# Softmax reciprocals taken before they are spread, and every low part subtracted on VectorE

## The chip, the cores and the metric

The kernel runs on one core of one Trainium2 chip. The metric is the device time of the program in microseconds; a profiled execution has besides its time a span, from the first to the last instruction of its trace. TensorE multiplies matrices, VectorE, ScalarE and GpSimd work on tiles in SBUF, and SyncE issues the loads.

## The reference

Two blocks follow each other on 256 tokens of width 1024, all in float32. The first has two layers over 256 latent and 256 context tokens. Each normalises, projects with `w_in`, runs three branches side by side (a gated MLP over chunks, an attention with 8 query and 2 key heads, and a two-way mLSTM scan), and projects with `w_out`. The second block has two layers too: an attention of 16 heads (`moba`) or a low-rank attention of 16 heads (`mla`), each followed by a feed-forward part with a short convolution.

```python
def _attend(q, k, v):
    s = jnp.einsum('bqkgd,bskd->bkgqs', q, k).astype(jnp.float32) * ATTN_SCALE
    p = jax.nn.softmax(s, axis=-1).astype(v.dtype)
    return jnp.einsum('bkgqs,bskd->bqkgd', p, v)
...
def conv_ffn(xn, w_gate, conv_w, conv_b, w_up, w_down):
    S = xn.shape[1]
    g = xn @ w_gate
    gp = jnp.pad(g, ((0, 0), (CONV_WIDTH - 1, 0), (0, 0)))
    gc = conv_b + sum(conv_w[j] * gp[:, j:j + S] for j in range(CONV_WIDTH))
    h = jax.nn.gelu(gc, approximate=False) * (xn @ w_up)
    return h @ w_down
```

## The kernel before

Activations lie transposed: features on the 128 partitions, tokens along the free axis, as eight tiles (`KT`) of 128 features. Each product of float32 matrices is made of three matmuls in a shorter format. `split` (L130) makes the high part of a tile by a cast on ScalarE and the low part by subtracting that cast from the tile, and `mm3` (L105) or `stream_on` (L120) adds high by high, low by high and high by low in one accumulator.

Weights come in pieces of up to 128x1024 by `fetch` (L145): `w_load` loads a piece into `st` (four buffers), and `w_split` makes `wh` on ScalarE and `wl`, the low part (five buffers each). `fetch` takes a key and looks it up in the table `POOL_LO` (L58). The table's digits say which pieces of that fetch have their low part subtracted on GpSimd; all others, and every fetch without a key, have it on VectorE. The feed-forward stages (`ffn`, L1320) fetch without a key.

In attention a softmax weight is left undivided. `attend` (L782) in the first block and `weights_of` (L1032) in the second take the exponentials and, with the same ScalarE instruction, their sums, one column per head, into `dn`. The division comes after the product with the values: `inv_rows` (L293) makes the reciprocals, repeated 64 times along the free axis, so that transposes on TensorE turn them into rows that lie like the heads' outputs. It is called 12 times in the first block with four heads (128x256), and eight times by `out_heads` (L1064) with eight columns (128x512). `out_heads` then copies the rows from PSUM, multiplies, and splits the heads' output; that split's low part is on GpSimd.

The order of the work in a stage is written out by hand in the strings of `PLAN` (L46), one letter and number for a step. On top of it the framework schedules the recorded instructions anew when the program is built, by a model of the engines' times, and each engine then runs its own list strictly in order. So a change of one instruction's engine shifts rows on all engines. The residual additions are L915 and L1083, the square sums L274, the output products' next splits L921 and L1006; the scan of the gate statistics is L610 and L613, the rope products L492 and L497.

Of the kernel before, what the change touches and what calls it, by code (L numbers as in the profile page):

```python
# [28 lines left out]
def _cols(*spans):  # L29
# [26 lines left out]
}  # L56

POOL_LO = {"g00": "1", "g03": "1", "g04": "01", "g05": "0", "g10": "1", "g11": "1", "g12": "1", "g13": "01",  # L58
# [4 lines left out]

FWD = [2, 3, 0, 1]
BWD = [3, 2, 1, 0]
# [3 lines left out]
def tile_two_blocks(ctx: ExitStack, tc: tile.TileContext, A, out, dbg=None):  # L69
    nc = tc.nc  # L70
    V, S, G, PE = nc.vector, nc.scalar, nc.gpsimd, nc.tensor
# [9 lines left out]
    def bank(tag):  # L81
        return psum.tile([128, 512], F32, name=tag)
# [47 lines left out]
    def split(hi, lo, src, lo_eng=None):  # L130
        S.copy(hi, src)  # L131
        (lo_eng or V).tensor_tensor(lo, src, hi.bitcast(F32), op=OP.subtract)  # L132

    def w_load(src):
        st = wpool.tile([128, src.shape[-1]], F32, name="st", bufs=4)
        load(st, src)
        return st

    def w_split(st, on_pool):
        hi = wpool.tile(list(st.shape), F32R, name="wh", bufs=5)  # L140
        lo = wpool.tile(list(st.shape), F32R, name="wl", bufs=5)
        split(hi, lo, st, G if on_pool else V)
        return hi, lo

    def fetch(src, pieces, key=None):  # L145
        r, a = [], 0
        for i, p in enumerate(pieces):
            r.append(w_split(w_load(src[:, a:a + p]), str(i) in POOL_LO.get(key, "")))
            a += p
# [5 lines left out]
    def transpose(o, i):  # L155
        last_tr[0] = PE.transpose(o, i, ident[:i.shape[0], :i.shape[0]]).ins  # L156
# [136 lines left out]
    def inv_rows(rr, cols):  # L293

        n = cols.shape[-1]
        rr = rr[:, :n * 64].rearrange("p (a b) -> p a b", b=64)
        V.reciprocal(rr, cols.unsqueeze(2).to_broadcast([128, n, 64]))  # L297
        pt = bank("tr")
        for p in range(n // 2):
            transpose(pt[:, p * 128:(p + 1) * 128], rr[:, 2 * p:2 * p + 2, :].rearrange("p a b -> p (a b)"))  # L300
        return pt[:, :n * 64]
# [9 lines left out]
    def first_layer(l, ncx, x, rc):  # L311
# [470 lines left out]
        def attend(t, i):  # L782
# [38 lines left out]
            if p:  # L821
                oj = obs[t][:, j * 256:(j + 1) * 256]
                S.copy(oj, inv_rows(T2(), dn[:, j * 4:j * 4 + 4]))
                V.tensor_tensor(oj, po[j][:, :256], oj, op=OP.mult)
# [144 lines left out]
    x, rc = first_layer(0, True, x0, None)  # L969
# [94 lines left out]
    def out_heads(sb, po, dn, oh, ol, g):  # L1064

        pt = inv_rows(sb.tile([128, 512], F32, name="rr2", bufs=1), dn[:, 8 * g:8 * g + 8])
        o = sb.tile([128, 2, 256], F32, name="ov", bufs=2)
        of = o.rearrange("p a b -> p (a b)")
        S.copy(of, pt)
        V.tensor_tensor(of, po, of, op=OP.mult)  # L1070
        split(oh[:, 2 * g:2 * g + 2, :], ol[:, 2 * g:2 * g + 2, :], o, G)

    def w_o_proj(name, src, oh, ol, first, nrm):
        w = first
# [12 lines left out]
    def moba(hh, hl, rc):  # L1087
# [68 lines left out]
        oh = sb2.tile([128, 8, 256], F32R, name="moh")  # L1156
        ol = sb2.tile([128, 8, 256], F32R, name="mol")
        steps["o"] = lambda g: out_heads(sb, ov[g], dn, oh, ol, g)
        for f_ in late_.split():
            steps[f_[0]](int(f_[1:]))  # L1160
# [6 lines left out]
    def mla(nrm):  # L1167
# [139 lines left out]
        def value_heads(g):  # L1307
            ov[g] = values_of(PTs, va, 4 * g)

        steps = {"k": keys_of, "q": queries_w, "h": weights, "u": lambda i: values(i, wv[i]), "v": value_heads,  # L1310
                 "o": lambda g: out_heads(sb, ov[g], dn, oh, ol, g)}
        for f_ in PLAN["mla"].split():
            steps[f_[0]](int(f_[1:]))
# [191 lines left out]
```

## Time and profile before

| | |
|---|---|
| median of 3 runs | 1150.46 us (1150.42 to 1152.39) |
| profiled execution | 1150.56 us, span 1148.8 us |
| TensorE busy | 1096.8 us, 95% of the span |
| VectorE busy | 772.9 us, 67% |
| ScalarE busy | 596.6 us, 52% |
| GpSimd busy | 295.6 us, 26% |
| weight low parts on VectorE | 211 instructions, 250.0 us |
| weight low parts on GpSimd | 61 instructions, 140.7 us |

TensorE is busy in nearly all of the span, so the table says little about where time can be won or lost; that is read from single waits. Busy times are of one execution. A busy TensorE is not always TensorE at its full clock.

### The profile page before, as it was taken

To read this page: it belongs to the slowest core of one execution; us is meant where nothing else is said; L and a number is where in the kernel's file an instruction comes from. 1 tells how busy PE (TensorE), PEld (TensorE's weight loads), DVE (VectorE), ACT (ScalarE), POOL (GpSimd) and SP (SyncE) were. 2 spreads that over 40 slices of the span, in tenths; PEclk is the share of its full clock that TensorE was granted. 3 is DMA by queue.
4 is the path that set the end of the run, shared out by engine and by line. 5 is a ranking of instruction groups with operands and counts; after the bars stand their busy time and mean duration, and the time that the engine had idled before them with its cause. 6 is when DMAs were issued, how large, how long until landed. Compare 5 with 4: busy or idle time off the path is not lost. (4 is left out here: it accounts for less than half of the span.)

```text
span 1148.8 us, 20497 instructions
## 1 busy us (share of the span) xinstructions
PE 1096.8 (95%) x7826; PEld 960.6 (84%) x7826; DVE 772.9 (67%) x1525; ACT 596.6 (52%) x1158; POOL 295.6 (26%) x283
## 2 busy tenths in 40 slices
PE   5999989999899899988999999999999989999997
PEld 3686777687677799887876899999998889999996
DVE  4774574666646766877576777776556877777653
ACT  4446543443435475554456565555447856555541
POOL 1350321321212725334222312221032331222100
PEclk9999999999899999999999999999999999999998
DMA  9624310534742243124442355556545325555561
GB/s 337 242 83 148 129 55 1 184 128 167 229 141 88 73 132 121 65 98 152 165 140 81 122 173 188 187 181 182 175 143 171 112 91 175 194 185 184 178 183 45
DMA packets 52610, 167.32 MB, mean 146 GB/s; under 512 B 6816, under 2 KB 10400, under 8 KB 52512
## 3 DMA queue, kind: packets, MB, share of 16 engines
q1 hardware_dynamic: 52512, 166.01, 43.4%
q8 instruction: 62, 1.02, 0.3%
q14 instruction: 36, 0.29, 0.1%
HBM read 164.41 MB, written 1.05 MB: 144 GB/s over the span
## 5 line engine op out<-in xcount | busy, mean ns | idle before, releaser
L131 ACT CAST wh<-st 128x1024 fp32r<-128x1024 f32 (+4 forms) x272 | 268.7, 992 | 202.4 <-PE acc L100 112.6
L132 DVE TENSOR_TENSOR wl<-st,wh 128x1024 fp32r<-128x1024 f32 (+4 forms) x211 | 250.0, 1187 | 110.6 <-ACT wh L131 106.2
L132 POOL TENSOR_TENSOR wl<-st,wh 128x1024 fp32r<-128x1024 f32 (+4 forms) x61 | 140.7, 2317 | 272.3 <-ACT wh L131 246.3
L100 PE MATMUL acc<-xyh,wh 128*128 128x512 f32 (+1 forms) x320 | 112.1, 351 | 6.3 <-DVE xres L915 4.4
L100 PE MATMUL acc<-xyl,wh 128*128 128x512 f32 (+1 forms) x320 | 111.3, 350 | 2.6 <-DVE xyl L132 2.6
L100 PE MATMUL acc<-xyh,wl 128*128 128x512 f32 (+1 forms) x320 | 111.1, 348 | 0.0
L100 PE MATMUL acc<-wh,xyh 128*128 128x512 f32 (+1 forms) x256 | 96.6, 377 | 4.9 <-DVE t L497 3.5
L100 PE MATMUL sc<-hl,wh 128*128 128x256 f32 x352 | 99.0, 281 | 0.0
L100 PE MATMUL sc<-hh,wl 128*128 128x256 f32 x352 | 99.0, 281 | 0.0
L100 PE MATMUL acc<-hl,wh 128*128 128x256 f32 x352 | 99.0, 281 | 0.0
L100 PE MATMUL acc<-ah,wh 128*128 128x256 f32 x352 | 99.0, 281 | 0.0
L100 PE MATMUL acc<-al,wh 128*128 128x256 f32 x352 | 99.0, 281 | 0.0
L100 PE MATMUL acc<-ah,wl 128*128 128x256 f32 x352 | 98.9, 281 | 0.0
L100 PE MATMUL sc<-hh,wh 128*128 128x256 f32 x352 | 98.9, 281 | 0.0
L100 PE MATMUL acc<-hh,wh 128*128 128x256 f32 x352 | 98.8, 281 | 0.0
L100 PE MATMUL acc<-hh,wl 128*128 128x256 f32 x352 | 98.8, 281 | 0.0
L100 PE MATMUL acc<-wh,xyl 128*128 128x512 f32 (+1 forms) x256 | 94.8, 370 | 0.0
L100 PE MATMUL acc<-wl,xyh 128*128 128x512 f32 (+1 forms) x256 | 94.3, 372 | 0.0
L100 PEld LDWEIGHTS acc<-xyh,wh 128*128 128x128 f32 x320 | 62.5, 195 | 15.1 <-issue 5.0
L100 PEld LDWEIGHTS acc<-xyl,wh 128*128 128x128 f32 x320 | 62.4, 196 | 10.1 <-DVE xyl L132 3.1
L100 PEld LDWEIGHTS acc<-xyh,wl 128*128 128x128 f32 x320 | 62.3, 195 | 7.0
L100 PEld LDWEIGHTS sc<-hl,wh 128*128 128x128 f32 x352 | 66.4, 189 | 0.0
(463 smaller groups left out, 2724.8 us busy)
## 6 DMA issues: line engine op xcount, KB each, us to landing
st<-w_gu SPq DMA_DIRECT2D x88, 512.0 KB, 3.8
st<-w_dn SPq DMA_DIRECT2D x32, 512.0 KB, 3.5
st<-w_in_t SPq DMA_DIRECT2D x24, 512.0 KB, 4.2
st<-w_in_f SPq DMA_DIRECT2D x24, 512.0 KB, 4.7
st<-a_w_qkv SPq DMA_DIRECT2D x24, 512.0 KB, 3.3
st<-w_ada SPq DMA_DIRECT2D x20, 512.0 KB, 3.4
st<-w_out SPq DMA_DIRECT2D x16, 512.0 KB, 4.3
st<-w_dn SPq DMA_DIRECT2D x16, 384.0 KB, 3.4
```

What stands on the lines that cost most here:

```text
L100: last_mm[0] = PE.matmul(o, lhsT, rhs, start=start, stop=stop).ins
L131: S.copy(hi, src)
L132: (lo_eng or V).tensor_tensor(lo, src, hi.bitcast(F32), op=OP.subtract)
```

## The change

Three edits. The table of pieces whose low part goes to GpSimd is emptied, so all 272 weight low parts are on VectorE. The low part of the heads' output in `out_heads` goes to VectorE as well. And `inv_rows` first takes the reciprocal of the sums in place, in `dn`, and then spreads it by a copy with the same broadcast input.

```diff
-POOL_LO = {"g00": "1", "g03": "1", "g04": "01", "g05": "0", "g10": "1", "g11": "1", "g12": "1", "g13": "01",
...
+POOL_LO = {}
...
         n = cols.shape[-1]
         rr = rr[:, :n * 64].rearrange("p (a b) -> p a b", b=64)
-        V.reciprocal(rr, cols.unsqueeze(2).to_broadcast([128, n, 64]))
+        V.reciprocal(cols, cols)
+        V.tensor_copy(rr, cols.unsqueeze(2).to_broadcast([128, n, 64]))
         pt = bank("tr")
...
-        split(oh[:, 2 * g:2 * g + 2, :], ol[:, 2 * g:2 * g + 2, :], o, G)
+        split(oh[:, 2 * g:2 * g + 2, :], ol[:, 2 * g:2 * g + 2, :], o)
```

The changed file is four lines shorter above `inv_rows` and three below its edit, so L132 becomes L128, L297 becomes L293 and L294, and L915 becomes L912.

VectorE at the end of `moba`, where the last groups of heads are divided, before (`rr` are the spread reciprocals, `mdn` the sums, `ov` the heads' output; ISA rows are the score rows of `weights_of`):

```order
L1039 ISA nb_6412 128x1
L297 RECIPROCAL rr_6381<-mdn 128x512
L1070 TENSOR_TENSOR ov<-pv,ov 128x512
L297 RECIPROCAL rr_6436<-mdn 128x512
L1070 TENSOR_TENSOR ov<-pv,ov 128x512
L1048 COPY PT_6421<-tr 128x384
L1070 TENSOR_TENSOR ov<-pv,ov 128x512
```

The same place in the changed program:

```order
L1036 ISA nb_6427 128x1
L294 COPY rr_6395<-mdn 128x512
L1067 TENSOR_TENSOR ov<-pv,ov 128x512
L293 RECIPROCAL mdn<-mdn 128x8
L294 COPY rr_6451<-mdn 128x512
L128 TENSOR_TENSOR mol<-ov,moh 128x512
L1067 TENSOR_TENSOR ov<-pv,ov 128x512
L1045 COPY PT_6436<-tr 128x384
L128 TENSOR_TENSOR mol<-ov,moh 128x512
L1067 TENSOR_TENSOR ov<-pv,ov 128x512
L128 TENSOR_TENSOR mol<-ov,moh 128x512
```

Each long reciprocal has become a short one and a copy, and the low parts `mol` stand in VectorE's list between the products.

VectorE in the output product of the second layer of the first block, before (`xres` is the residual, `tg` and `sqa` the square sums, `xyl` the low part of the next stage's input):

```order
L915 SCALAR_TENSOR_TENSOR xres<-acc,mod_84,xres 128x256
L274 TENSOR_TENSOR tg<-tg 128x256
L921 SCALAR_TENSOR_TENSOR xyl<-xres,g_5172,xyh 128x256
L274 TENSOR_TENSOR sqa<-sqa,sqb 128x256
L274 TENSOR_TENSOR tg<-tg 128x256
L921 SCALAR_TENSOR_TENSOR xyl<-xres,g_5172,xyh 128x256
L915 SCALAR_TENSOR_TENSOR xres<-acc,mod_84,xres 128x256
L274 TENSOR_TENSOR sqa<-sqa,sqb 128x256
```

The same place in the changed program:

```order
L912 SCALAR_TENSOR_TENSOR xres<-acc,mod_84,xres 128x256
L270 TENSOR_TENSOR tg<-tg 128x256
L918 SCALAR_TENSOR_TENSOR xyl<-xres,g_5184,xyh 128x256
L270 TENSOR_TENSOR sqa<-sqa,sqb 128x256
L128 TENSOR_TENSOR wl<-st,wh 128x1024
L270 TENSOR_TENSOR tg<-tg 128x256
L918 SCALAR_TENSOR_TENSOR xyl<-xres,g_5184,xyh 128x256
L912 SCALAR_TENSOR_TENSOR xres<-acc,mod_84,xres 128x256
L270 TENSOR_TENSOR sqa<-sqa,sqb 128x256
```

One `wl` row of 128x1024 has come in per step of one block of features.

VectorE where the second layer's keys end and its queries begin, before (`kl` is the keys' low part; the rows that read `acc` are those that free TensorE's accumulators):

```order
L497 TENSOR_TENSOR t_3619<-t_3615,tabk 128x2x16 x4
L132 TENSOR_TENSOR kl<-tr,kh 128x2x128
L499 TENSOR_TENSOR k_3617<-t_3618,t_3619 128x2x64
L537 TENSOR_REDUCE ssq<-t_3706 128x8
L492 TENSOR_TENSOR t_3715<-acc,tabq 128x512
L497 TENSOR_TENSOR t_3716<-acc,tabq 128x8x16 x4
```

The same place in the changed program:

```order
L494 TENSOR_TENSOR t_3627<-t_3623,tabk 128x2x16 x4
L128 TENSOR_TENSOR wl<-st,wh 128x1024
L128 TENSOR_TENSOR kl<-tr,kh 128x2x128
L496 TENSOR_TENSOR k_3625<-t_3626,t_3627 128x2x64
L128 TENSOR_TENSOR wl<-st,wh 128x1024 x2
L534 TENSOR_REDUCE ssq<-t_3714 128x8
L489 TENSOR_TENSOR t_3723<-acc,tabq 128x512
L494 TENSOR_TENSOR t_3724<-acc,tabq 128x8x16 x2
```

Three `wl` rows now stand ahead of the rows that read the accumulator.

## Rows read from the trace of the kernel before

**Rows 1.** Timeline, first layer's output product: start us, us, engine line op [idle <-releaser]

```profile
289.12 0.68 DVE L132 TENSOR_TENSOR xyl<-xres,xyh 128x512 fp32r<-128x512 f32 x1
...
294.85 5.12 POOL L132 TENSOR_TENSOR wl<-st,wh 128x1024 fp32r<-128x1024 f32 x2 [13.52 <-ACT wh L131]
...
295.32 2.44 DVE L132 TENSOR_TENSOR xyl<-xres,xyh 128x512 fp32r<-128x512 f32 x1 [1.97 <-ACT xyh L131]
...
297.69 2.30 DVE L202 TENSOR_TENSOR mod<-mod,c_b_ada 128x8 f32<-128x8 f32 x1
...
300.65 0.80 PE L100 MATMUL acc<-xyl,wh 128*128 128x512 f32 x1 [2.64 <-DVE xyl L132]
```

**Rows 2.** Timeline, gate statistics of the first layer.

```profile
159.32 1.79 DVE L613 TENSOR_TENSOR mrow<-Mr,be 4x1 f32<-4x1 f32 x1
...
161.74 0.25 DVE L613 TENSOR_TENSOR mrow<-Mr,be 4x1 f32<-4x1 f32 x2
...
162.34 2.39 POOL L132 TENSOR_TENSOR wl<-st,wh 128x1024 fp32r<-128x1024 f32 x1 [1.24 <-ACT wh L131]
...
162.68 2.12 DVE L613 TENSOR_TENSOR mrow<-Mr,be 4x1 f32<-4x1 f32 x2
...
166.80 1.14 PE L156 MATMUL pv<-c_ident,Mr 4*128 4x4 f32 x7 [2.57 <-DVE mrow L613]
```

**Rows 3.** Timeline, second layer, from keys to queries.

```profile
382.98 2.68 DVE L497 TENSOR_TENSOR t<-t,tabk 128x32 f32<-128x32 f32 x4
...
388.32 0.53 PE L100 MATMUL acc<-wh,xyh 128*128 128x512 f32 x1 [3.46 <-DVE t L497]
```

**Rows 4.** Timeline, second layer's output product.

```profile
510.42 4.97 POOL L132 TENSOR_TENSOR wl<-st,wh 128x1024 fp32r<-128x1024 f32 x2 [15.47 <-issue]
...
513.08 2.60 DVE L274 TENSOR_TENSOR tg<-tg 128x256 f32<-128x256 f32 x1
...
516.61 0.36 PE L100 MATMUL acc<-xyh,wh 128*128 128x256 f32 x1 [2.07 <-DVE xres L915]
...
517.00 0.43 DVE L274 TENSOR_TENSOR tg<-tg 128x256 f32<-128x256 f32 x1 [0.21 <-ACT tg L272]
...
517.40 0.48 DVE L921 SCALAR_TENSOR_TENSOR xyl<-xres,g,xyh 128x256 fp32r<-128x256 f32 x1
...
524.87 0.36 PE L100 MATMUL acc<-xyh,wh 128*128 128x256 f32 x1 [2.29 <-DVE xres L915]
```

**Rows 5.** Busy times by stretch: stretch, length, each engine, PEclk, DMA share, GB/s.

```profile
160.00:175.00 15.00, 12.07 (x49) 9.77 (x49) 11.66 (x35) 4.74 (x10) 5.65 (x5) 0.77 0.28 105
295.00:310.00 15.00, 11.21 (x36) 8.37 (x36) 9.46 (x11) 5.99 (x8) 6.85 (x3) 0.77 0.67 227
520.00:535.00 15.00, 12.71 (x75) 11.69 (x74) 11.60 (x16) 6.51 (x12) 6.10 (x3) 0.89 0.39 140
```

**Rows 6.** Timeline, ends of the two attention mixers.

```profile
625.15 0.63 PE L156 MATMUL tr<-c_ident,rr 128*128 128x128 f32 x4 [1.34 <-DVE nb L1037]
...
912.50 3.35 DVE L297 RECIPROCAL rr<-ldn 128x512 f32<-128x512 f32 x1
...
925.06 0.63 PE L156 MATMUL tr<-c_ident,rr 128*128 128x128 f32 x4 [1.00 <-DVE rr L297]
```

**Rows 7.** Groups by form on VectorE, whole span: busy us, mean ns | idle before.

```profile
L132 DVE TENSOR_TENSOR wl<-st,wh 128x1024 fp32r<-128x1024 f32 x175 | 220.1, 1259 | 91.9 <-ACT wh L131 88.9
...
L297 DVE RECIPROCAL t<-dn 128x256 f32<-128x256 f32 x12 | 21.0, 1751 | 14.6 <-ACT P L810 14.6
...
L340 DVE CAST xyh<-t 128x512 fp32r<-128x512 f32 x7 | 2.9, 412 | 0.0
...
L733 DVE RECIPROCAL den<-den 128x4 f32<-128x4 f32 x12 | 2.1, 174 | 0.3
```

**Rows 8.** Chain of waits that ended last, first feed-forward stage: start us, us.

```profile
676.58 2.85 PE acc L100 x24
```

**Rows 9.** Waits by releaser: us in total, times, longest.

```profile
DVE wl L132 <- ACT wh L131: 106.2, 122, 4.7
```

4 rows, old and new, of the table POOL_LO are left out of this document.

## Prediction

> **What bounds the kernel now.** I read the busy times by stretch first, then what TensorE waited for, then the timeline around each wait. TensorE is what the end follows: it is busy in nearly all of the span, and inside both feed-forward stages its matmuls stand back to back. Those stages call the weight fetch without a key, so they had no subtract on GpSimd before either, and the change leaves them alone. What can be won lies in the waits of TensorE in the other stages and in the half clock that follows a long wait. Read the timelines as pairs: a GpSimd subtract, and beside it a VectorE instruction that takes far longer than its form needs.
>
> In the first layer's output product [rows 1], GpSimd runs two subtracts from 294.85 for 5.12 us. The VectorE split of 128x512 that began at 295.32 takes 2.44 us; the same form took 0.68 at 289.12. The 128x8 add after it takes 2.30 us. The last split comes behind both, and TensorE waits 2.64 us for it. In the gate statistics [rows 2], one 4x1 add takes 1.79 us, and two take 2.12 us beside the GpSimd subtract of 162.34, where two took 0.25 just before it; TensorE waits 2.57 us. At the second layer's query chunk [rows 3], four rope products take 2.68 us, and TensorE waits 3.46 us for a reader of its accumulator. In the second layer's output product [rows 4], an add takes 2.60 us against 0.43 four microseconds later, and TensorE waits 2.07 and 2.29 us for the residual add that frees its accumulator. After three of these places the granted clock is at the lower of its two levels, 1.2 of 2.4 GHz, for a time: it averages 0.77, 0.77 and 0.89 of full speed over 15 us stretches that hold them [rows 5], which is 15 x 0.23 = 3.45 us twice and 15 x 0.11 = 1.65 us.
>
> At the end of both attention mixers the long reciprocal is what TensorE waits for [rows 6]: 128x512 takes 3.35 us on VectorE, and four transposes, the first at 625.15 and the last at 925.06, wait 1.34 (for a score row queued behind the reciprocal), 0.89, 1.02 and 1.00 us, 4.25 us together.
>
> **The change, part by part.** *The reciprocals.* Twenty calls become forty: a reciprocal of 128x4 or 128x8 and a copy that spreads it. The trace has a 128x4 reciprocal, 174 ns; the 128x8 one I take at the same 0.17 [rows 7]. A spreading copy does not occur. From below, the 128x512 cast from SBUF to SBUF takes 0.41; from above, a two-input instruction of 128x512 takes 0.68 [rows 1]. I take 0.54, the middle, as neither end has a stride of zero in its input; for 128x256 half, 0.27. So 128x256 goes from 1.75 to 0.44 and 128x512 from 3.35 to 0.71, which over 12 and 8 calls is 15.7 + 21.1 = 36.8 us of VectorE. Most of that lies beside matmuls and is worth nothing by itself. On the path are the four waits: each is shorter than the 2.64 us that its reciprocal loses, so all of it goes. **Term A: 4.2 us gained** (2 if the order puts score work ahead of the copies, 6 if the later steps of the mixers move up too).
>
> *The head low parts.* Eight subtracts of 128x512 go from GpSimd to VectorE, where that form takes 0.68 us [rows 1]. They lie in the same chain, where VectorE now has 2.6 us more room per group. Zero, the cover being that room; without it 8 x 0.68 = 5.4 us, of which the last in each mixer, 1.4 us, would be seen.
>
> *The weight low parts.* 61 subtracts leave GpSimd, where one of 128x1024 takes 2.56 us (a pair 5.12, [rows 1]), and join 211 on VectorE, where that form takes 1.26 [rows 7]. VectorE gains at most 61 x 1.26 = 77 us of work, a little less since some are narrower. Against it stands the stretch that vanishes. At the places above GpSimd subtracts added 1.76 and about 2.1 us (rows 1, two subtracts; the small add taken at 0.2), 1.87 (rows 2, one), and 2.17 to one add alone (rows 4): close to 2 us per subtract, more than the 1.26 us of doing it on VectorE.
>
> The Trainium skill, page "SBUF — State Buffer", section "Who interferes with whom", has GpSimd and a VectorE instruction with two SBUF inputs exclude each other, the later one blocked until the first is done. The split at 295.32 ended just after the first subtract and the add at 297.69 with the second, so the trace agrees [rows 1]. The rule has a side that speaks against the change: where VectorE began first it is GpSimd that waits, VectorE lost nothing, and the move costs the whole 1.26 us; that is the case that the far end of term F stands for.
>
> Place by place, with the new order:
> - Second layer's output product: before, two subtracts stood on GpSimd beside each of two steps. Now each step has one wl row on VectorE (wl is the low part of a weight). A step is then four instructions of 128x256, which take 0.43 to 0.48 us undisturbed [rows 4], and a subtract: 4 x 0.45 + 1.26 = 3.06 us, against 2.85 us for its 24 matmuls of 128x256 (as many of that form in the first feed-forward stage, [rows 8]). VectorE falls behind 0.2 us a step, 1.6 us in eight. Waits of 4.36 and clock of 1.65 go, 1.6 comes. **Term B: 4.4 gained** (0 to 6).
> - First layer's output product: the late pair was 2.44 + 2.30 + 0.68 = 5.42 us; now two wl rows stand among these three, 0.68 + 0.2 + 0.68 + 2 x 1.26 = 4.1. The wait for the split shrinks by 1.3 and part of the clock loss goes with it. **Term C: 2.0** (from -1, if a wl row waits for its load, to 6.1, the whole wait and 3.45 of clock).
> - Gate statistics: the stretch of the adds goes, 1.66 + 1.87 = 3.5 us, and three instructions of some 0.43 us now stand between the scans. TensorE's wait shrinks by 2.3, and I give a third of the clock, 1.2. **Term D: 3.5** (0 to 6).
> - Query chunk: before, the four small rope products alone take 2.68 us. Now three wl rows, 3 x 1.26 = 3.8 us, stand ahead of the instruction that frees the accumulator. **Term E: 0** (-3 to 5).
> - The other moved subtracts (some 45) stand where VectorE has room: even in the three stretches of [rows 5], stretched instructions counted, it is busy 9.5 to 11.7 of 15 us. If one in twenty is seen at 1.26 us: **term F: 3 lost** (0 to 15, the far end if one in four is).
>
> The sum: 4.2 + 4.4 + 2.0 + 3.5 + 0 - 3 = 11.1 us. The profiled execution took 1150.56 us, its span 1148.8 and 1.76 around it; the median shown is 1150.46, so the same base. **Forecast 1139.5 us.**
>
> **Rivals.** *All of it goes.* If VectorE keeps its room everywhere, A stays and B, C, D reach their upper ends, and E's wait vanishes: 4.2 + 6 + 6.1 + 6 + 3.5 = 25.8, with nothing lost: 1124.8 us. For it: nearly all of these waits have a GpSimd subtract or a long reciprocal beside them. Against it: the three wl rows in front of E, and the 3.06 us step in B.
>
> *Nothing moves.* The contention becomes a queue of the same length, as in E, everywhere; only A is left, less F: 1149.4 us. For it: stretch and moved work are of like size. Against it: in B and D the new rows take less than the stretch.
>
> *Slower.* VectorE's queue is in order, and a wl row that waits for its ScalarE cast holds all behind it. Today 122 of its waits are for such a cast, 106.2 us together, 0.87 each [rows 9]. With GpSimd no longer taking those waits, 61 more at 0.87 are 53 us of standing VectorE; what is late next is whatever frees an accumulator. If TensorE sees a third, 17.7 us, in place of F, the time is 1150.56 - 14.1 + 17.7 = 1154.2 us. It decides from 14.1 / 61 = 0.23 us seen per moved subtract. For it: in the second layer's query chunk wl rows stand right before the accumulator's readers. Against: the scheduler lays a row where its cast is to be done, and 211 subtracts live there already.
>
> **How the numbers follow.** The forecast has 0.56, all of it goes 0.22, nothing moves 0.10, slower 0.12. A measurement of this kernel can tell about 0.2%, 2.3 us, from no change. The forecast's own range, from the terms' bounds taken a few at a time, is 1130 to 1147, faster throughout. So faster 0.78, same 0.10, slower 0.12. The range for 8 in 10 reaches to the quick rival and to the slow one: 1119 to 1154.
>
> **What would show it.** Right: no VectorE instruction of 2 us in the non-feed-forward stages; wl on VectorE x272 at close to 1.23; reciprocals of 0.17 and copies between 0.41 and 0.68; the four waits for rr gone; clock at full speed after the second layer's output product. Wrong: TensorE waits in those stages whose releaser is a wl row or what stands behind one on VectorE, VectorE idle before wl rows far above 106 us, or new places of half clock. The forecast fails if the new order of the rows, which shifts on every engine, opens waits that no row here shows.

## The result, and the profile after

The changed kernel takes 1136.15 us (median of 4 runs, 1135.77 to 1137.94), the kernel before 1150.44 beside it. The ratio is 0.988, with a 95% interval of 0.9862 to 0.9898, so 14.3 us are gained where 11.1 were forecast. The profiled execution took 1135.77 us, 14.8 less than that of before. Busy time, first part of the page of the changed kernel:

```profile
PE 1091.0 (96%) x7826; PEld 957.0 (84%) x7826; DVE 748.3 (66%) x1614; ACT 596.7 (53%) x1158; POOL 149.0 (13%) x214
```

GpSimd's time has halved, and VectorE, which took all of that work over, is busy 25 us less than before. Its groups by form say why:

```profile
L128 DVE TENSOR_TENSOR wl<-st,wh 128x1024 fp32r<-128x1024 f32 x228 | 280.5, 1233 | 115.4 <-ACT wh L127 110.2 <-PE acc L96 1.8
...
L294 DVE COPY t<-dn 128x256 f32<-128x256 f32 x12 | 3.5, 290 | 0.4
...
L293 DVE RECIPROCAL dn<-dn 128x4 f32<-128x4 f32 x12 | 2.1, 176 | 8.5 <-ACT P L807 8.5
...
L294 DVE COPY rr<-mdn 128x512 f32<-128x512 f32 x4 | 1.7, 426 | 1.3 <-PE tr L152 1.1
...
L293 DVE RECIPROCAL mdn<-mdn 128x8 f32<-128x8 f32 x4 | 0.8, 197 | 1.1 <-ACT sm L1039 1.1
```

A reciprocal of 3.35 us [rows 6] has become one of 0.20 and a copy of 0.43. A weight subtract is 1.23 where it was 1.26. What TensorE waited for, and the wait for casts that [rows 9] gave:

```profile
PE tr L96 <- DVE t L270: 13.9, 1, 13.9
PE acc L96 <- DVE rb L1113: 4.5, 2, 4.2
...
DVE wl L128 <- ACT wh L127: 132.0, 144, 9.9
```

The first is the wait for the first loads, at the start of the program, which was 12.7 us before. Two names are gone from the top: the residual add (2.07 and 2.29 us in [rows 4]) and the spread rows `rr` of [rows 6]. One has come up to the top: `rb`, the rope product in `moba`, with 4.2 us in one wait. Single instructions of the same places, timeline of the changed kernel:

```profile
162.34 0.21 DVE L610 TENSOR_TENSOR mrow<-Mr,be 4x1 f32<-4x1 f32 x2
...
164.29 0.22 PE L152 MATMUL pv<-c_ident,Mr 4*128 4x4 f32 x1 [0.68 <-DVE Mr L607]
...
254.81 0.44 PE L96 MATMUL pv<-va,t 128*128 128x65 f32 x2 [1.31 <-DVE t L712]
...
294.26 0.68 DVE L128 TENSOR_TENSOR xyl<-xres,xyh 128x512 fp32r<-128x512 f32 x1
294.87 0.16 DVE L198 TENSOR_TENSOR mod<-mod,c_b_ada 128x8 f32<-128x8 f32 x1
...
296.81 0.50 PE L96 MATMUL acc<-xyl,wh 128*128 128x512 f32 x1 [1.22 <-DVE xyl L128]
...
380.44 0.47 PE L96 MATMUL acc<-wh,xyh 128*128 128x512 f32 x1 [1.89 <-DVE t L494]
...
504.25 1.22 DVE L128 TENSOR_TENSOR wl<-st,wh 128x1024 fp32r<-128x1024 f32 x1
505.39 0.41 DVE L270 TENSOR_TENSOR tg<-tg 128x256 f32<-128x256 f32 x1
...
506.85 1.21 DVE L128 TENSOR_TENSOR wl<-st,wh 128x1024 fp32r<-128x1024 f32 x1
...
527.89 1.23 DVE L128 TENSOR_TENSOR wl<-st,wh 128x1024 fp32r<-128x1024 f32 x1
...
530.33 1.22 DVE L128 TENSOR_TENSOR wl<-st,wh 128x1024 fp32r<-128x1024 f32 x1 [0.74 <-ACT wh L127]
531.47 0.15 DVE L951 TENSOR_TENSOR r1c<-r1c,rcx 128x2 f32<-128x2 f32 x1
531.75 0.48 DVE L1089 TENSOR_SCALAR mtab<-c_rope,r1c 128x128 f32<-128x128 f32 x2
...
533.64 0.77 PE L96 MATMUL acc<-wh,xyh 128*128 128x512 f32 x1 [4.25 <-DVE rb L1113]
```

The pairs of [rows 1], [rows 2] and [rows 4] are apart: the split of 128x512 takes 0.68 in place of 2.44, the 128x8 add 0.16 in place of 2.30, two 4x1 adds 0.21 in place of 2.12, the 128x256 add 0.41 in place of 2.60. TensorE's waits there fall from 2.64 to 1.22, from 2.57 to 0.68, and to nothing; the one of 3.46 [rows 3] falls to 1.89. Last comes the wait that has grown: two weight rows, at 527.89 and 530.33, stand in the short chain that makes `moba`'s rope table `mtab` from the square sums, and TensorE's accumulators come free only after it. The weight row at 530.33 ends just before `r1c`, which scales the table. The same wait before the change, timeline of before:

```profile
543.72 0.47 PE L100 MATMUL acc<-wh,xyh 128*128 128x512 f32 x1 [1.41 <-DVE rb L1116]
```

The granted clock by stretch (columns as in [rows 5]), changed kernel:

```profile
160.00:175.00 15.00, 13.79 (x73) 10.93 (x72) 12.23 (x45) 5.76 (x13) 1.40 (x2) 1.00 0.32 105
250.00:265.00 15.00, 13.48 (x95) 11.36 (x92) 10.39 (x29) 4.20 (x11) 2.49 (x3) 0.77 0.19 63
290.00:305.00 15.00, 13.71 (x61) 10.68 (x61) 11.64 (x21) 7.32 (x10) 0.00 (x0) 1.00 0.83 307
380.00:395.00 15.00, 14.56 (x77) 12.61 (x78) 11.81 (x29) 6.94 (x14) 6.64 (x5) 1.00 0.31 109
...
515.00:530.00 15.00, 14.40 (x78) 12.05 (x76) 8.79 (x18) 6.97 (x11) 2.11 (x3) 1.00 0.47 159
...
532.00:547.00 15.00, 13.36 (x51) 10.90 (x52) 5.01 (x10) 3.93 (x5) 2.51 (x2) 0.77 0.18 58
```

The three places of [rows 5] are at full clock. So is the query chunk, behind the wait of 1.89 us; before the change it had half clock for a time too, a fourth place, which [rows 5] does not have:

```profile
380.00:395.00 15.00, 11.54 (x47) 9.12 (x46) 12.91 (x25) 5.16 (x9) 13.31 (x8) 0.89 0.29 92
```

That was 15 x 0.11 = 1.65 us. Two other places have half clock in their stead, behind the waits of 1.31 and 4.25 us: 15 x 0.23 = 3.45 us each.

Where the time came from shows at three places that both programs reach. At the restart of `moba`'s projection the changed kernel is 543.72 - 533.64 = 10.1 us ahead, and loses 3.45 of that to the clock right behind it. Then two pieces of TensorE's work in the chain that ended last, one in each feed-forward stage, changed kernel:

```profile
659.59 2.85 PE acc L96 x24
...
941.63 2.82 PE acc L96 x24
```

and before:

```profile
670.89 2.85 PE acc L100 x24
...
956.66 2.82 PE acc L100 x24
```

It is 11.3 us ahead in the first feed-forward stage and 15.0 in the second. So the first block with the projection gave 10.1 - 3.45 = 6.7 us, the rest of `moba` 4.6 and `mla` 3.7, in these two executions; the feed-forward stages gave nothing. Such a split is rough. The kernel with the heads' edit alone (below) has on VectorE and GpSimd the same rows in the same order as the kernel before up to that restart, and yet reached it 4.0 us sooner, with less half clock on the way:

```profile
539.73 0.47 PE L100 MATMUL acc<-wh,xyh 128*128 128x512 f32 x1 [1.41 <-DVE rb L1116]
```

So a time at one place of one execution is uncertain by some 4 us.

### The profile page after: what moved, and what is told of

The parts are those of the page before. It is cut to its first block, busy times and chain, and to the rows that moved or that the text cites. A ratio compares the mean times of both kernels' runs of the same rounds, so it can differ in the third digit from the quotient of the medians.

```text
span 1134.0 us, 20510 instructions
## 1 busy us (share of the span) xinstructions
PE 1091.0 (96%) x7826; PEld 957.0 (84%) x7826; DVE 748.3 (66%) x1614; ACT 596.7 (53%) x1158; POOL 149.0 (13%) x214
## 4 chain that ended last, share of the span: by engine, by line
PE 44%; issue 6%; ACT 1%; DVE 1%; DMA 0%; POOL 0%; POOLq 0%; DVEq 0%; ACTq 0%
PE acc L96 27%; PE sc L96 13%; PE tr L152 2%; PE pv L96 1%; ACT wh L127 1%; DMA st<-b_w_uv 0%; DVE wl L128 0%; DVE hg L1383 0%; PE tr L96 0%; POOL t L1351 0%; DVE rb L1113 0%; ACT sm L1038 0%; ACT sm L1039 0%; ACT Q L1287 0%; DVE hres L1080 0%
## 5 line engine op out<-in xcount | busy, mean ns | idle before, releaser
L128 DVE TENSOR_TENSOR wl<-st,wh 128x1024 fp32r<-128x1024 f32 (+4 forms) x272 | 315.3, 1162 | 137.5 <-ACT wh L127 132.0
L96 PE MATMUL acc<-xyh,wh 128*128 128x512 f32 (+1 forms) x320 | 109.5, 343 | 2.7 <-ACT xyh L127 2.1
L96 PE MATMUL acc<-xyl,wh 128*128 128x512 f32 (+1 forms) x320 | 108.2, 341 | 1.2 <-DVE xyl L128 1.2
L96 PE MATMUL acc<-xyh,wl 128*128 128x512 f32 (+1 forms) x320 | 108.8, 340 | 0.0
L96 PEld LDWEIGHTS sc<-hh,wh 128*128 128x128 f32 x352 | 66.4, 189 | 0.0
L96 PEld LDWEIGHTS acc<-hh,wl 128*128 128x128 f32 x352 | 66.4, 189 | 0.0
```

Of the source, the lines that this page charges most:

```text
L96: last_mm[0] = PE.matmul(o, lhsT, rhs, start=start, stop=stop).ins
```

## The experiments

Three theories were set against each other. **Contention:** GpSimd's subtracts stretch VectorE's rows, and the gain beyond the four waits is that stretch gone. **Room:** the reciprocals' 37 us of VectorE carry the whole. **Order:** the scheduler happened on a better order. Each ratio is to the kernel before on the same chip.

**Each edit alone, on the kernel before.** The reciprocals:

```diff
-        V.reciprocal(rr, cols.unsqueeze(2).to_broadcast([128, n, 64]))
+        V.reciprocal(cols, cols)
+        V.tensor_copy(rr, cols.unsqueeze(2).to_broadcast([128, n, 64]))
```

> The kernel before with only the reciprocals changed (short reciprocal, then a spreading copy); low parts stay where they were. Theory 1, contention: the change's gain of 14.3 us is made of the four waits for the spread rows at the ends of the two attention mixers, 4.25 us, and for the rest of GpSimd subtracts that no longer stretch VectorE's rows; this edit alone gives 4.25 us, 1146.2 us (1144 to 1148), and the waits of 2 to 3.5 us at the output products, the gate statistics and the query chunk are all still there. Theory 2, room: the 37 us of VectorE time that the reciprocals give back are what the whole gain rests on, and the low parts only move into that room; then this edit alone gives 10 us or more, 1140 us or less. Theory 3, order: the gain is that of another order of the rows on all engines, with no cause of its own; then this run may lie anywhere, above 1150 too, and its waits are at new places.

Measured 1140.97 us, ratio 0.9916 (0.9902 to 0.993): 9.0 us, twice the contention theory's number and a little under the room theory's. At the first layer's output product, timeline of this kernel:

```profile
294.44 2.75 POOL L132 TENSOR_TENSOR wl<-st,wh 128x1024 fp32r<-128x1024 f32 x1 [3.10 <-ACT wh L131]
...
294.84 2.37 DVE L202 TENSOR_TENSOR mod<-mod,c_b_ada 128x8 f32<-128x8 f32 x1
...
297.87 0.50 PE L100 MATMUL acc<-xyl,wh 128*128 128x512 f32 x1 [1.54 <-DVE xyl L132]
```

No reciprocal stands there, and the 128x8 add is as stretched as ever. But the pair of subtracts of [rows 1] has been pulled apart by the new order, one stands here, the wait is 1.54 us in place of 2.64, and the clock over the stretch of [rows 5] is 1.00 in place of 0.77. The gate statistics are alike: other rows stand beside the subtracts, and the wait is 0.87 us in place of 2.57. So part of this gain is taken from the same waits as terms C and D.

The weights:

```diff
-POOL_LO = {"g00": "1", "g03": "1", "g04": "01", "g05": "0", "g10": "1", "g11": "1", "g12": "1", "g13": "01",
...
+POOL_LO = {}
```

> The kernel before with only the table of pieces emptied: all 272 weight low parts on VectorE, the long reciprocals kept, the heads' low parts still on GpSimd. Theory 1, contention: 14.3 less the 4.25 us of the four waits, so about 10 us gained, 1140.4 us (1138 to 1143); the four waits of 0.9 to 1.3 us for the spread rows stay, and no VectorE row beside a weight subtract takes 2 us. Theory 2, room: without the reciprocals' 37 us VectorE has 77 us of work more and no room for it: 1150 to 1155 us. Theory 3, order: anywhere, with the waits at new places.

Measured 1144.88 us, ratio 0.9952 (0.9939 to 0.9964): 5.1 us gained, half of the contention theory's number, and the room theory's loss did not come. TensorE's waits of this kernel:

```profile
PE acc L96 <- DVE rb L1112: 5.7, 2, 5.4
PE sc L96 <- DVE nb L1035: 3.8, 2, 2.4
```

The wait at `moba`'s projection is there too, so it comes from the weights; and score rows (`nb`) queued behind the long reciprocals now cost 3.8 us, where one of 1.34 stood [rows 6]. In this execution the restart of `moba`'s projection comes at 533.46 us, 10.3 ahead, with a half clock of 3.45 behind it, and the second feed-forward piece at 951.27, 5.4 ahead: so some 1.4 us are lost again in the mixers as long as the long reciprocals are there.

The heads' low parts:

```diff
-        split(oh[:, 2 * g:2 * g + 2, :], ol[:, 2 * g:2 * g + 2, :], o, G)
+        split(oh[:, 2 * g:2 * g + 2, :], ol[:, 2 * g:2 * g + 2, :], o)
```

> The kernel before with only the eight low parts of the heads' outputs moved from GpSimd to VectorE. Theory 1, contention: these eight lie in the chain that ends with the long reciprocals; VectorE takes 0.68 us for each where GpSimd takes some 1.3, and the four waits are for rows that stand ahead of them: 0 to 1 us gained, 1149.4 to 1150.4 us. Theory 2, room: with the long reciprocals still there the eight rows are late by their own length, up to 1.4 us lost, 1150.4 to 1151.8 us. Theory 3, order: nearly all rows stand as before, so nothing beyond 1 us either.

Measured 1151.32 us, ratio 1.0014 (1.0004 to 1.0024): 1.4 us lost, as the room theory had it. The waits for the spread rows, in this kernel:

```profile
PE tr L156 <- DVE rr L297: 5.6, 3, 2.4
```

They were 2.9 us before. The three edits alone add up to 9.0 + 5.1 - 1.4 = 12.7 us, and together they gave 14.3. The difference of 1.6 lies within the intervals, so it is not shown that they help one another.

**The reciprocals of the first block alone.**

```diff
+        if n == 4:
+            V.reciprocal(cols, cols)
+            V.tensor_copy(rr, cols.unsqueeze(2).to_broadcast([128, n, 64]))
+        else:
+            V.reciprocal(rr, cols.unsqueeze(2).to_broadcast([128, n, 64]))
```

> The kernel before with the short reciprocal and the copy only where a call has four columns, which are the twelve calls of the first block; the eight of the mixers keep the long reciprocal, all low parts stay where they were. The reciprocals alone gave 9.0 us; up to the mixers that kernel had gained 5.6 on the kernel before. If the two halves do not touch each other, 4.8 us are gained here, 1145.2 us (1144 to 1146.5), with the waits for the spread rows at the ends of the mixers still there. By the prediction's own account, which gave the first block's reciprocals nothing, 1150 us.

Measured 1147.51 us (12 runs, 1145.74 to 1150.9), ratio 0.9977 (0.9964 to 0.999): 2.4 us, half of what was expected and more than the prediction's nothing. By difference the mixers' eight reciprocals would be worth 9.0 - 2.4 = 6.6 us, some 2 us either way by the two intervals. The trace of the kernel with all reciprocals divides it otherwise:

```profile
538.19 0.47 PE L100 MATMUL acc<-wh,xyh 128*128 128x512 f32 x1 [1.48 <-DVE rb L1117]
```

That is 5.5 us ahead at `moba`'s projection, and its second feed-forward piece, at 946.97, is 9.7 ahead: 4.2 for the mixers, what term A has. So the first block gave 2.4 to 5.5 us and the mixers 4.2 to 6.6; nearer the runs do not tell.

**Another order and nothing else**, on the kernel before.

```diff
+        V.tensor_copy(cols, cols)
         V.reciprocal(rr, cols.unsqueeze(2).to_broadcast([128, n, 64]))
```

> The kernel before with one small VectorE copy more ahead of each of the twenty long reciprocals: the sums copied onto themselves, 0.17 us each, which changes no result and moves the rows around as another order would. If the gains of the other kernels have their own causes, this one has the same waits and 0 to 2 us more, 1150 to 1152 us. If an order alone is worth several us either way, it lies outside 1148 to 1153, with waits gone or new ones come.

Measured 1150.3 us (12 runs, 1147.16 to 1152.96), ratio 0.9998 (0.9983 to 1.0012). This disturbance of the order is worth nothing. It is one order among many, and the reciprocals moved more of VectorE's rows, so it speaks against the order theory without ending it.

**GpSimd's work in halves**, on the kernel before.

```diff
+        half = st.shape[-1] // 2
+        for c in (slice(0, half), slice(half, None)) if on_pool else (slice(None),):
+            (G if on_pool else V).tensor_tensor(lo[:, c], st[:, c], hi[:, c].bitcast(F32), op=OP.subtract)
```

> The kernel before, each of the 61 GpSimd subtracts made as two of half the width; all the rest as it was. If a VectorE row has to wait until the GpSimd instruction that runs is done, its longest wait is halved: no small VectorE row beside a weight subtract takes much over 1.3 us, the waits at the output products and the gate statistics lose some 40%, and 3 to 6 us are gained, 1144 to 1147 us. If what counts is how long GpSimd works in all, whatever its pieces, the waits stay: within 1.5 us of 1150.

Measured 1144.38 us, ratio 0.9945 (0.9926 to 0.9963): 5.5 us gained, inside the number. Timeline of this kernel:

```profile
508.73 1.52 DVE L277 TENSOR_TENSOR tg<-tg 128x256 f32<-128x256 f32 x1
...
512.22 0.36 PE L100 MATMUL acc<-xyh,wh 128*128 128x256 f32 x1 [0.91 <-DVE xres L918]
...
519.39 0.36 PE L100 MATMUL acc<-xyh,wh 128*128 128x256 f32 x1 [1.19 <-DVE xres L918]
```

and its groups by form on GpSimd:

```profile
L145 POOL TENSOR_TENSOR wl<-st,wh 128x512 fp32r<-128x512 f32 x106 | 144.5, 1389 | 190.9 <-ACT wh L142 148.1 <-issue 24.8 <-PE tr L159 14.0
```

GpSimd works on the low parts no less than before (144.5 us here, and 14.4 for narrower pieces, against 140.7), and yet the stretched add falls from 2.60 to 1.52 and the two waits of 2.07 and 2.29 [rows 4] to 0.91 and 1.19. What a VectorE row pays is the GpSimd instruction that is running, and that is what the halves shorten. The Trainium skill, page "SBUF — State Buffer", section "Who interferes with whom", has a VectorE instruction with two SBUF inputs and a GpSimd instruction that reads SBUF exclude each other. The trace agrees: 1.52 us beside pieces of 1.39.

**The subtracts put back as idle work**, on the changed kernel.

```diff
+            if str(i) in ALSO_LO.get(key, ""):
+                G.tensor_tensor(st, st, r[-1][0].bitcast(F32), op=OP.subtract)
```

> The changed kernel, with the 61 GpSimd subtracts put back as idle work: for the pieces of the old table VectorE makes the low part as in the changed kernel, and after it GpSimd subtracts the same cast from the same piece in place, where nobody reads it; the piece's buffer is held until then, as it was before. The output is not touched. Theory 1, contention: VectorE's rows are stretched again by up to 2 us per subtract and the piece buffers come free later; the waits at the output products and the gate statistics come back and the waits for the short reciprocals do not: 6 to 12 us lost against the changed kernel, 1142 to 1148 us. If the stretch were not what cost the time (theory 2 or 3), GpSimd's idle work changes nothing beyond the order: within 2 us of 1136.2.

Measured 1191.95 us, ratio 1.036 (1.0346 to 1.0375): 56 us lost against the changed kernel, far beyond either number. VectorE is busy 829.0 us with the same 1614 instructions, 80.7 more, 1.3 for each subtract. Its wait for casts is hardly longer, 134.2 us against 132.0: its rows are stretched, not late. And the waits of [rows 1], [rows 2] and [rows 3] are back, as the contention theory has it: 3.30 us at the gate statistics (0.68 in the changed kernel), 4.56 at the first layer's output product (1.22), and 10.93 at the second layer's query chunk (1.89). Timeline of this kernel:

```profile
302.81 0.79 PE L102 MATMUL acc<-xyl,wh 128*128 128x512 f32 x1 [4.56 <-DVE xyl L134]
...
387.25 6.92 POOL L153 TENSOR_TENSOR st<-st,wh 128x1024 f32<-128x1024 f32 x3
...
390.56 2.42 DVE L498 TENSOR_TENSOR t<-t,tabk 128x128 f32<-128x128 f32 x1
...
397.19 0.77 PE L102 MATMUL acc<-wh,xyh 128*128 128x512 f32 x1 [10.93 <-DVE tmq L176]
```

VectorE works without a gap from 383.53 to 397.13, and beside the three idle subtracts its rows are stretched: this rope product takes 2.42 us (0.29 at 373.13 in the changed kernel), and a weight row of 128x544 takes 2.66 (0.71). So the run shows the stretch, and that TensorE waits for it. It does not give the price of the contention in the kernel before, since VectorE makes the weight low parts here as well, and half clock behind the waits comes on top (mean clock 0.972 against 0.991). The piece buffers are also held longer, but ScalarE's casts waited 8.4 us for loads, against 6.8, so little of the loss can come from there.

**Halves with the short reciprocals** and the heads' low parts on VectorE (the diffs above together).

> The short reciprocals and the heads' low parts on VectorE as in the changed kernel, but the 61 weight low parts left on GpSimd, each in two halves. Halving alone gave 5.5 us and the reciprocals alone 9.0. If the gain of the moved weights is the shorter blocking of VectorE's rows, halves give most of it too and the two add up: 1135 to 1138 us. If it is that no GpSimd subtract stands in a chain at all, the halves stay behind: 1139 to 1141 us. VectorE has 65 us less work here than in the changed kernel, so if its load were what bounds, it would come out below 1134 us.

Measured 1137.38 us, ratio 0.9883 (0.9866 to 0.9901), the same as the changed kernel's 0.988. Either way of shortening the block gives the same, and 61 weight rows less on VectorE buy nothing that shows.

**The heads' low parts back on GpSimd**, in the changed kernel (the third diff reversed).

> The changed kernel with the eight low parts of the heads' outputs back on GpSimd. On the kernel before, moving them to VectorE alone cost 1.4 us, because they stood ahead of a long reciprocal. By the prediction they cost nothing next to short ones, since VectorE has 2.6 us more room per group: within 1 us of the changed kernel, 1135.5 to 1137 us. If they cost their length there too, 1134.8 us; if GpSimd subtracts in that chain cost more than they save, 1137 us and more.

Measured 1138.65 us (1135.54 to 1140.31), ratio 0.9888 (0.9872 to 0.9905). The interval holds the changed kernel's 0.988, so nothing is told apart here; the loss of 1.4 us that the edit alone had is at any rate not there.

**The new wait.** First the two weight rows moved behind the rope products that free the first accumulator, in the changed kernel:

```diff
+            with after(freed[0]):
+                return w_split(st, False)
...
+                if i == t == 0:
+                    freed[0] = last.ins
...
+        w = {0: fetch_q(0), 1: fetch_q(1, range(3))}
...
+                w[1].append(piece(1, 3))
```

> The changed kernel, with two weight low parts moved on VectorE: the last piece of the second moba projection and the first of the third are issued behind the rope products that free the first accumulator, where they stood in the chain from the square sums to the rope table. If these two rows of 1.2 us each in that chain are what makes the new wait of 4.25 us at moba's first projection, 2.2 to 2.4 us of it go, and some of the 3.4 us of half clock behind it: 1130.5 to 1134 us. If something else on the chain (the GpSimd powers, TensorE's own order of the square sums) ends it, nothing is gained: 1135.5 to 1137 us.

Measured 1136.67 us, ratio 0.9881 (0.9861 to 0.99): nothing, and the wait is 4.92 us. Timeline of this kernel:

```profile
528.33 0.16 DVE L951 TENSOR_TENSOR r1c<-r1c,rcx 128x2 f32<-128x2 f32 x1 [0.81 <-POOL r1c L168]
531.42 0.48 DVE L1089 TENSOR_SCALAR mtab<-c_rope,r1c 128x128 f32<-128x128 f32 x2 [2.93 <-DMA c_rope<-rope]
```

The chain is 3.1 us shorter, as meant (`r1c` at 528.33, not 531.47). But the table `c_rope` that it scales has only just landed; its load stands behind eleven weight pieces in SyncE's queue, is issued at 526.59 and takes 4.7 us to land. Two things ended the wait at about the same time. As what TensorE waited for, the trace of the changed kernel shows the VectorE rows alone; that the load was issued at 527.60 there and took 4.1 us to land stands only among its DMA issues.

So the load was made early, into the tile of the first block's rope table, which is dead by then:

```diff
-    rope2 = const("rope2")
+    rope2 = late["ropeq"]
+    nc.sync.dma_start(rope2, A["rope2"])
```

> The changed kernel, with the rope table of moba loaded into the tile of the first block's rope table, which is read for the last time long before, so that the load is issued early; no row of TensorE, ScalarE or GpSimd moves. Moving the two weight low parts out of the chain gave nothing (1136.67 us), because the rope table itself landed just as late: VectorE then waited 2.93 us for it. If two things end that wait at the same time, taking away the late load alone gives nothing either: 1135.5 to 1137 us, with the wait of 4 to 5 us still there and the two weight rows in front of the table. If the load alone is what counts, 3 us or more are gained, 1133 us or less.

Measured 1135.91 us, ratio 0.9856 (0.9833 to 0.9879), the wait 4.15 us: alone this does not help either. Then both:

> The changed kernel with both edits: the rope table loaded early, and the two weight low parts behind the rope products that free the first accumulator. If these two are all that stands in that chain, the table is made at the end of the last GpSimd power, some 3 us sooner; TensorE's wait falls from 4.25 to 1 to 1.5 us, and the half clock behind it (3.4 us) goes with it, since a wait of that length at the query chunk is not followed by any: 1130 to 1133 us. If the clock falls nonetheless, 1133 to 1134 us; if a third thing ends the wait, 1135 to 1137 us.

Measured 1134.43 us (5 runs, 1127.92 to 1137.35), ratio 0.9857 (0.984 to 0.9874). Timeline of this kernel:

```profile
254.06 0.44 PE L96 MATMUL pv<-va,t 128*128 128x65 f32 x2 [1.31 <-DVE t L712]
...
525.88 0.48 DVE L1090 TENSOR_SCALAR mtab<-c_rope_lat,r1c 128x128 f32<-128x128 f32 x2
...
527.77 0.47 PE L96 MATMUL acc<-wh,xyh 128*128 128x512 f32 x1 [2.02 <-DVE rb L1121]
```

and its busy times by stretch:

```profile
246.00:261.00 15.00, 13.48 (x121) 11.14 (x121) 11.84 (x36) 5.79 (x15) 2.68 (x3) 1.00 0.18 49
526.00:541.00 15.00, 12.07 (x56) 9.76 (x56) 11.18 (x17) 5.93 (x7) 3.53 (x2) 1.00 0.51 156
```

The wait falls by 2.2 us, from 4.25 to 2.02, and this execution has full clock behind it. It is the lowest median of all kernels here, but its interval overlaps the changed kernel's, and by ratio it equals the kernel with the early load alone (0.9856), where the wait stayed. That it beats the changed kernel is not shown.

## Why the prediction was right, point by point

**The forecast.** 1139.5 us was forecast, 1136.15 came, inside both ranges. The mechanism at the places that it named is the one that the runs show: without the GpSimd subtract beside it a VectorE row is back to what its form needs, halving the subtract halves the block, and TensorE's waits follow. That the sum came so close is in part luck: terms A to E were sized too small and the loss of term F too, and the errors cancelled.

**Term A, the reciprocals: 4.2 forecast, about 9.0 measured alone.** The prices were right (0.62 us for the pair against 0.71, 0.47 against 0.44), and the four waits are gone. The step that failed is "Most of that lies beside matmuls and is worth nothing by itself": the first block's twelve alone gave 2.4 us, clear of noise. What the part above 4.25 consists of was seen in two places, a pair of subtracts pulled apart and other rows beside them in the gate statistics; that it is the room in VectorE's list that lets the order do this is argued, not shown.

**Head low parts: zero forecast, and nothing told apart in the changed kernel.** Without the cover they cost 1.4 us, the number that the prediction gave for that, as the kernel with this edit alone shows.

**Term B, the second layer's output product: 4.4 forecast.** This and what follows compares one execution of each kernel. Both waits and the half clock went, 4.36 + 1.65 = 6.0 us, the upper end. The VectorE step was forecast at 3.06 us and took 2.60 (504.25 to 506.85): a row starts some 0.07 us before the one ahead of it ends, and 0.40 is nearer than 0.45, so no backlog builds up.

**Term C, 2.0 forecast:** the wait fell by 1.42, close to the 1.3 forecast, but the whole 3.45 of clock came back, 4.9 together. **Term D, 3.5 forecast:** 1.89 of wait (2.3 forecast) and again all of the 3.45, 5.3 together. What was mis-sized is the share of the clock, set at a part and a third. **Term E, zero forecast:** the wait fell by 1.57, and the half clock behind it went, 1.65, which the prediction had not seen: 3.2 together. Three weight rows stand ahead of the accumulator's reader as foreseen, but the rope products before them had lost more to GpSimd, 2.19 us in the four of [rows 3] (0.49 undisturbed) and 1.88 in the one before them (2.16 in place of 0.28).

**Term F, 3 lost forecast.** The loss is larger and sits in two places that no row had pointed to: `moba`'s projection, where the wait grew by 4.25 - 1.41 = 2.84 us, a new wait of 1.31 us at 254.81, and a half clock of 3.45 us behind each. That is 11.1 us given back. The prediction named this kind of failure in its last sentence, without a place or a price. Terms B to F as measured make 6.0 + 4.9 + 5.3 + 3.2 - 11.1 = 8.3 us, where the restart of `moba`'s projection shows 6.7; 1.2 of the difference is the first wait of the program, 13.9 us against 12.7, which the edits don't touch.

**The signs.** Those of being right came, but for one: a weight row of VectorE at 577.33 still takes 2.16 us, beside GpSimd's rope addition of 577.12, and no wait of TensorE's follows. Two of the signs of being wrong came as well, a wait for what stands behind weight rows (`rb`) and new places of half clock.

**The rivals.** *Nothing moves* fell: the weights alone gave 5.1 us, so a queue of VectorE's own rows is not as bad as the block. *Slower* fell: VectorE's wait for casts rose from 106.2 to 132.0 us, 25.8 more and not 53, and of TensorE's waits behind weight rows only the one at `moba`'s projection is longer than before. *All of it goes* (1124.8) was missed by 11.4 us, though the places named gave nearly their upper ends: it is the new places that keep the time from there.

**What stays open.** The idle subtracts show the stretch, but at a price that can't be carried to the kernel before, so the contention there was priced by halving alone. How the reciprocals' 9.0 us divide between the first block and the mixers is known to some 2 us only. A GpSimd load that touches no buffer was not tried, nor any cure for the wait at 254.81.

## What to carry to other kernels

A long instruction on a second engine that shares memory with a first costs the first one's small rows up to its whole length. If it can't be taken away, cut it in pieces: halves gave as much here as moving all of it. Run each part of a change by itself as well: here the reciprocals alone gave 9.0, the weights 5.1, and the heads lost 1.4, which the time of the whole does not tell. A wait that a trace puts down to one releaser may have a second just behind; here the wait shrank only when both were gone.

## What the runs showed of the hardware that had not been expected

The granted clock differs between executions of one program more than most of these edits do. Executions of the kernel with both last edits took from 1127.92 us, at a mean clock of 0.998, to 1137.35, at 0.989. The same wait of 1.31 us is followed by a stretch at 0.77 in the changed kernel (254.81) and by full clock in that one (254.06); of the two kernels with one of these edits, that with the early load has 0.77 there and the other full clock. So a wait's price is its length, and at times 3.45 us more; a difference of 3 us between two profiles says little before the clock by stretch has been read.

A copy with a stride of zero in its input is hardly slower for it: 426 ns for 128x512, next to 412 for the cast of that form [rows 7].
